# The prompt's output projection of a hybrid decoder step, cut by half the columns and a quarter of the rows instead of a quarter and a half, inside the page steps

## The chip, the cores and the metric

One Trainium2 chip, one of its cores. The metric is the device time of one launch in microseconds; the median of 3 runs of the kernel before is 806.1 us (802.2 to 810.11). The engines are called TensorE (PE, and PEld for its weight loads), VectorE (DVE), ScalarE (ACT), GpSimd (POOL) and SyncE (SP).

## What is computed

One step of a decoder layer for a prompt of 512 tokens and for 8 sample sequences of 4 tokens each, which look back on 4096 cached tokens. Each layer projects the input, runs a recurrent group and an attention group with three branches (compressed, selected, sliding window), gates both, concatenates them and projects the result back. What the change touches is this:

```
s = jnp.einsum('bkgtd,bjkd->bkgtj', q, kc[:, :, 0]) * ATTN_SCALE        # compressed_attn, sample: keys from the cache pages
...
o = g[0] * o_c + g[1] * o_s + g[2] * o_w
o = o.transpose(0, 3, 1, 2, 4).reshape(B, T, N_WIDTH).astype(y_r.dtype) * jax.nn.silu(gate_n)
return jnp.concatenate([y_r, o], axis=-1) @ w_out                       # mixer_out
...
y = x + mixer_out(y_r, o_c, o_s, o_w, gl, gate_n, w_out)                # prompt_layer: 512 x 1024 times 1024 x 1024
...
y_prompt = rms_norm(y_p, final_g)
```

## The kernel before

The launch has three stages: the input projection and the recurrent group (to about 330 us), the prompt's attention with the rest of the recurrent group (to about 536 us), and then the stage that the change touches.

**Page steps.** The samples' cache is read page by page by an indirect DMA that GpSimd issues (`load_page`, L1328 to L1332). A step s = 8b + i takes page i of sequence b, 64 steps in all; I call the eight steps of a sequence a batch. Four page buffers hold the pages (NPAGE), and step s issues the load of page s + 4 when its own page is no longer read. The order of the work on TensorE, VectorE, ScalarE and GpSimd is written out by hand (`manual_schedule`, L1714), and each engine runs its instructions in that order. SyncE's queue, which carries the plain loads and stores, is ordered by a scheduler.

In each step `keys` (L1690) turns the page's selected keys (`ks_set`, L1394) and compressed keys (`kc_set`, L1373): four TensorE transposes of 128 x 128 each into one of three PSUM banks, from which ScalarE copies the former (`kts`) and VectorE the latter (`ktc`; in step 3 ScalarE). `keep_values` copies the page's values away (`vt`, on ScalarE in even steps, on VectorE in odd ones). `scores` multiplies the compressed keys of two pages in every odd step (`kc_mm`, L1384 to L1391), the selected keys of four pages in steps 3 and 7 (`ks_mm`, L1407), and at the end of a batch copies the compressed scores out of PSUM (`top1`, `sc`, L1414).

`chain` and `chain_early` then do for sequence b - 1, spread over the steps of batch b, what follows from its scores: the selection (`top2`, `top2b`, `top3`: L1420 to L1448, with the block scores `bs` on VectorE), the penalty (`top4`, L1455 to L1467, whose matmuls at L1457 need `bs`, and VectorE's copies `pe` at L1460), the softmax (L1476 to L1486), the transposes of the weights (`weights`, L1492, copied as `p` by ScalarE and VectorE), the products with the values (L1504, L1519, L1530) and their reduction (`values_r`, `Rc`, L1512).

**The prompt's output projection** runs in the same steps. The product is made in split precision: a weight piece is copied to a high part by ScalarE and its remainder made by GpSimd (`o_split`, L1551, tile WHL), a piece of the gated input G is split the same way by ScalarE and VectorE (`o_prep`, L1561, tile CHL), and TensorE adds high x high, low x high and high x low in PSUM (`o_mm`, L1567). There are 8 units u of 256 columns (u // 2) and half of the rows (u % 2), each with 8 calls of `o_mm`: four blocks i of 128 tokens, each in two parts c of two row tiles, six matmuls of 256 columns a call. After the second part VectorE adds the bank to Y (L1575), and after the second half of the rows ScalarE sums the squares (L1577). `output_step` (L1581) gives a unit nine steps: its split in the first, a call in each of the other eight, and the piece for a call is made one step before it:

```
        u, r = divmod(s, 9)
        if r == 0: o_split(u)
        if r < 8:  o_prep(u, r)
        if r:      o_mm(u, r - 1)
```

So 72 steps are needed: 64 page steps hold units 0 to 6 and the split of unit 7, and the eight calls of unit 7 lie in the eight steps after the last page. With each second call of unit 7 `final(i)` (L1595 to L1602) normalises a token block: two small VectorE steps, a power on GpSimd, one VectorE product with the gain vector `fgt`, and the store. The gain vector is loaded by unit 7's split over the weight buffer WS.

**The tail.** After the last page step the chain of the last sequence runs in eight steps without pages, each followed by `output_step`; then `join` combines the branches of all sequences (L1610 to L1658) and the samples' projection and normalisation end the launch (L1758 to L1769). The weights for it (WO) are loaded into the page buffers.

The functions that the diff touches, with the lines of the profile:

## Time and profile before

| | |
|---|---|
| median of 3 runs | 806.1 us (802.2 to 810.11) |
| profiled execution | 805.09 us |
| its span, first to last instruction | 803.3 us |
| mean granted TensorE clock | 0.948 of 2.4 GHz |
| busy: TensorE, VectorE, ScalarE, GpSimd | 719.6, 515.4, 341.8, 293.5 us |

Times are microseconds from the span's start unless marked ns. A row of a timeline gives the start, the busy time, the engine, the line, the operation, the tile written and the tiles read, the shapes and the number of instructions merged; in brackets stands how long the engine had been idle and what ended that. Matmuls are pipelined and their ends modelled, so that the distance of two starts says more than one duration.

### The profile page before, as it was taken

The numbers are of one execution on the slowest core, as the hardware profiler recorded it, in microseconds if no ns is written. First come the engines' busy times: TensorE is split into PE (matmuls) and PEld (weight loads), VectorE is DVE, ScalarE is ACT, GpSimd is POOL, SyncE is SP. The second block draws the span as 40 slices with busy tenths as digits, with TensorE's granted clock in tenths as the row PEclk, the third lists the DMA queues.
The fourth block names the chain that finished last, engine by engine and source line by source line (L and its number), as shares of the span: only waits on it lengthen the run. The fifth ranks groups of instructions, "written<-read, shape, count | busy, mean of one in ns | idle before, by whom it ended". The sixth has DMA issues, their size and how long they took to land.

```text
span 803.3 us, 17119 instructions
## 1 busy us (share of the span) xinstructions
PE 719.6 (90%) x6922; PEld 602.2 (75%) x6922; DVE 515.4 (64%) x1236; ACT 341.8 (43%) x731; POOL 293.5 (37%) x323
## 2 busy tenths in 40 slices
PE   3997988998899999699999999988989999998775
PEld 2896977888787999598888787665757766676553
DVE  7687587779921520867766665855776666667653
ACT  5335635542021223234544343455554664656420
POOL 5276566554231164500011023224443554434100
PEclk9998998999799899769999999999999999999977
DMA  7733233265373133311115100389888889898841
GB/s 212 264 90 99 63 95 95 53 169 111 81 157 88 29 105 79 119 21 27 28 27 133 27 8 1 127 294 369 301 326 286 304 321 312 299 344 321 253 126 60
DMA packets 103912, 125.01 MB, mean 156 GB/s; under 512 B 59085, under 2 KB 90551, under 8 KB 95386
## 3 DMA queue, kind: packets, MB, share of 16 engines
q1 hardware_dynamic: 94074, 56.48, 26.4%
q0 software_dynamic: 9216, 67.11, 23.0%
q8 instruction: 54, 0.88, 0.4%
q10 hardware_dynamic: 544, 0.33, 0.2%
q14 instruction: 24, 0.20, 0.1%
HBM read 112.81 MB, written 15.26 MB: 159 GB/s over the span
## 4 chain that ended last, share of the span: by engine, by line
PE 61%; DVE 18%; DMA 10%; issue 5%; ACT 4%; POOL 2%; SPq 1%; POOLq 0%; DVEq 0%; ACTq 0%
PE bx L366 16%; DMA pg<-in_cache_kv_dram,idx 5%; PE bn L1256 2%; PE bn L1571 2%; PE ba L1391 2%; PE bt L1001 2%; PE bn L1250 2%; PE bt L1398 2%; PE bn L1519 2%; PE bn L1504 2%; PE bt L1009 1%; DVE LT L566 1%; PE bn L1231 1%; DVE CHL L1565 1%; PE bt L1381 1%
## 5 line engine op out<-in xcount | busy, mean ns | idle before, releaser
L366 PE MATMUL bx<-xh,WR 128*128 128x272 f32 x992 | 182.9, 300 | 2.6 <-POOL WR L360 2.3
L366 PEld LDWEIGHTS bx<-xh,WR 128*128 128x128 f32 x992 | 149.7, 197 | 6.2 <-POOL WR L360 2.7
L366 PE MATMUL bx<-xl,WR 128*128 128x272 f32 x496 | 110.5, 299 | 0.0
L1332 POOL DMA_INDIRECT pg<-in_cache_kv_dram,idx x64 | 62.6, 978 | 119.1 <-PE bn L1530 18.3
L360 POOL TENSOR_TENSOR WR<-WA,WR 128x1024 fp32r<-128x1024 f32 x31 | 76.1, 2454 | 70.5 <-ACT WR L114 70.3
L366 PEld LDWEIGHTS bx<-xl,WR 128*128 128x128 f32 x496 | 83.3, 198 | 0.9
L1571 PE MATMUL bn<-WHL,CHL 128*128 128x256 f32 x384 | 64.8, 304 | 3.9 <-DVE CHL L1565 2.6
L1571 PEld LDWEIGHTS bn<-WHL,CHL 128*128 128x128 f32 x384 | 51.7, 195 | 8.6 <-DVE CHL L1565 4.3
L114 ACT ACTIVATE WR<-WA 128x1024 fp32r<-128x1024 f32 x31 | 32.7, 1056 | 57.6 <-PE bx L366 26.7
L1382 DVE COPY ktc<-bt 128x512 f32<-128x512 f32 x38 | 26.1, 687 | 32.4 <-PE bt L1381 32.4
L1025 POOL TENSOR_TENSOR std<-st,DC 128x512 f32<-128x512 f32 x7 | 7.3, 1049 | 99.5 <-DVE st L1051 37.6
L1565 DVE TENSOR_TENSOR CHL<-G,CHL 128x256 fp32r<-128x256 f32 x64 | 32.2, 503 | 17.1 <-ACT CHL L114 17.1
L1235 ACT ACTIVATE pr<-bn,nm 128x128 f32<-128x128 f32 (+3 forms) x57 | 28.8, 507 | 26.1 <-PE bn L1250 12.1
L1391 PE MATMUL ba<-ktc,WA 128*32 128x255 f32 x512 | 34.0, 383 | 6.3 <-DVE ktc L1382 4.7
L114 ACT ACTIVATE kts<-bt 128x512 f32<-128x512 f32 x43 | 25.5, 593 | 31.1 <-PE bt L1398 31.1
L1234 DVE TENSOR_REDUCE nm<-bn 128x1 f32<-128x128 f32 (+3 forms) x57 | 26.0, 461 | 7.1 <-PE bn L1233 6.7
L1555 POOL TENSOR_TENSOR WHL<-WA,WHL 128x512 fp32r<-128x512 f32 x16 | 21.1, 1338 | 25.7 <-ACT WHL L114 25.7
L1398 PEld LDWEIGHTS bt<-ident,pg 128*128 128x128 f32 x172 | 18.6, 140 | 15.0 <-issue 10.0
L114 ACT ACTIVATE vt<-pg 128x1024 f32<-128x1024 f32 x28 | 29.4, 1048 | 0.0
L1398 PE MATMUL bt<-ident,pg 128*128 128x128 f32 x172 | 27.4, 282 | 2.1 <-DMA pg<-in_cache_kv_dram,idx 2.0
L1256 PE MATMUL bn<-ps,VP 128*64 128x128 f32 x320 | 27.4, 287 | 1.2 <-ACT ps L114 1.0
L1391 PEld LDWEIGHTS ba<-ktc,WA 128*32 128x32 f32 x512 | 14.3, 109 | 18.0 <-DVE ktc L1382 5.2
(544 smaller groups left out, 1774.7 us busy)
## 6 DMA issues: line engine op xcount, KB each, us to landing
WA<-in_w_in_dram SPq DMA_DIRECT2D x23, 512.0 KB
WA<-in_w_in_dram SPq DMA_DIRECT2D x16, 256.0 KB
vt<-in_cache_kv_win_dram SPq DMA_DIRECT2D x8, 512.0 KB
out_dram<-in_cache_kv_win_dram SPq DMA_DIRECT2D x8, 508.0 KB
...
```

The costliest lines, as they stand in the source:

```text
L114: return act(o, i, AF.Copy, scale=scale)
L360: ptt(lo[:, :, :n], src[:, :, :n], h[:, :, :n], op=OP.subtract)
L366: mm(z[:, u, 0:HT], w[:, t, :], x[u][:, t, :], start=first, stop=last)
L1234: red(nm[:, k:k + 1], S[:, 0:n], axis=AX.X, op=OP.max, negate=True)
L1235: act(pr[:, k, 0:n], S[:, 0:n], AF.Exp, bias=nm[:, k:k + 1], accum_out=l2[:, k:k + 1])
L1256: mm(OT[64 * k:64 * k + 64, g, :], VP[:, br, t0 + t, 64 * k:64 * k + 64], ps[:, (2 * t + k) * P:(2 * t + k + 1) * P], start=False, stop=(b ...
L1332: nc.gpsimd.indirect_dma_start(out=t, out_offset=None, in_=cache_rows, in_offset=bass.IndirectOffsetOnAxis(ap=idx[:, 2 * b + c_t:2 * b + c ...
L1382: (acopy if i == 3 and b else cp)(KCT[b, q][:, :, c_t, :], pt.rearrange("p (t c) -> p t c", t=4))
L1391: mm(SCB[r, 0:255], QW[:, 4 * q + t, m, :], kt[:, t].rearrange("p a c -> p (a c)")[:, m:m + 255], start=(q == 0 and t < 2), stop=(q == 3 a ...
L1398: tp(pt[:, t * P:(t + 1) * P], PG[b, i][:, t, 2, :], ident)
L1565: tt(CHL[c][:, 1], cat, CHL[c][:, 0], op=OP.subtract)
L1571: mm(YB[:, 0:256], CHL[c][:, x, t], WHL[:, w, 2 * c + t], start=(c + t + x + w == 0), stop=(c + t == 2 and w == 1))
```

## The change

The projection goes by half the columns (512, h = u // 4) and a quarter of the rows (two row tiles, r = u % 4). A unit has four calls, one for each token block, of six matmuls of 512 columns; the bank is added to Y after each. `OSTEP` names the steps of the calls: the odd steps for units 0 to 5, and steps 49 to 52 and 54 to 57 for units 6 and 7. The splits come at steps 0, 8, 16, 24, 32, 40, 48 and 53, and the four `final(i)` at steps 59 to 62, so that nothing of it is left after the last page. In `keys` the compressed keys are transposed before the selected ones.

```diff
-    WHL = w2.tile([P, 2, 4, 256], F32R, name="WHL")
+    WHL = w2.tile([P, 2, 2, 512], F32R, name="WHL")
...
-    WS = WA[:, 1024:2048].rearrange("p (t c) -> p t c", t=4)
-    def load_wo(w, n, cols, c0):
-        if n < 4:
-            nc.sync.dma_start(w, dram(w_out, n * P * D + c0, [[D, P], [P * D, 4], [1, cols]]))
+    WS = WA[:, 1024:2048].rearrange("p (t c) -> p t c", t=2)
+    def load_wo(w, r, cols, c0):
+        if r < 2:
+            nc.sync.dma_start(w, dram(w_out, 2 * r * P * D + c0, [[D, P], [P * D, 2], [1, cols]]))
...
     def o_load(u):
-        load_wo(WS, 4 * (u % 2), 256, 256 * (u // 2))
+        load_wo(WS, u % 4, 512, 512 * (u // 4))
     def o_split(u):
-        for c in range(2):
-            t = slice(2 * c, 2 * c + 2)
+        for t in range(2):
             acopy(WHL[:, 0, t], WS[:, t])
             ptt(WHL[:, 1, t], WS[:, t], WHL[:, 0, t], op=OP.subtract)
...
-    def o_prep(u, n):
-        i, c = n // 2, n % 2
-        cat = G[:, 4 * (u % 2) + 2 * c:4 * (u % 2) + 2 * c + 2, i * P:(i + 1) * P]
-        acopy(CHL[c][:, 0], cat)
-        tt(CHL[c][:, 1], cat, CHL[c][:, 0], op=OP.subtract)
-    def o_mm(u, n):
-        (q, h), (i, c) = divmod(u, 2), divmod(n, 2)
+    def o_prep(u, i):
+        cat, hl = G[:, 2 * (u % 4):2 * (u % 4) + 2, i * P:(i + 1) * P], CHL[i % 2]
+        acopy(hl[:, 0], cat)
+        tt(hl[:, 1], cat, hl[:, 0], op=OP.subtract)
+    def o_mm(u, i):
+        h, r = divmod(u, 4)
         for t in range(2):
             for x, w in ((0, 0), (1, 0), (0, 1)):
-                mm(YB[:, 0:256], CHL[c][:, x, t], WHL[:, w, 2 * c + t], start=(c + t + x + w == 0),
-                   stop=(c + t == 2 and w == 1))
-        if c:
-            y = Y[i][:, 256 * q:256 * q + 256]
-            tt(y, YB[:, 0:256], y, op=OP.add)
-            if h:
-                act(YB[:, 256:512], y, AF.Square, accum_out=ssq[:, i, q:q + 1])
-            if u == 7:
-                final(i)
+                mm(YB, CHL[i % 2][:, x, t], WHL[:, w, t], start=(t + x + w == 0), stop=(t == 1 and w == 1))
+        y = Y[i][:, 512 * h:512 * h + 512]
+        tt(y, YB, y, op=OP.add)
+        if r == 3:
+            act(YB, y, AF.Square, accum_out=ssq[:, i, h:h + 1])
+    OSTEP = {}
+    for u in range(8):
+        for i in range(4):
+            OSTEP[8 * u + 2 * i + 1 if u < 6 else 48 + 5 * (u - 6) + i + 1] = (u, i)
     def output_step(s):
-        u, r = divmod(s, 9)
...
+        if s in (0, 8, 16, 24, 32, 40, 48, 53):
+            o_split(len([x for x in (8, 16, 24, 32, 40, 48, 53) if x <= s]))
+        if s + 1 in OSTEP:
+            o_prep(*OSTEP[s + 1])
+        if s in OSTEP:
+            o_mm(*OSTEP[s])
+        if 59 <= s < 63:
+            final(s - 59)
...
     def keys(b, i):
+        kc_set(b, i)
         ks_set(b, i)
-        kc_set(b, i)
...
         for i in range(8):
             chain_early(B - 1, i)
             chain(B - 1, i)
-            output_step(8 * B + i)
```

The loads of WO for the samples' projection use the new `load_wo` and move the same bytes.

On TensorE, the first three steps of a batch in the middle of the page steps, before (L1398 are the selected keys' transposes, L1381 the compressed keys', L1571 a call of the projection, L1420 and L1442 matmuls of the selection, L1391 the compressed scores, L1455 and L1457 the penalty):

```order
L1398 MATMUL bt_68<-ident,pg 128x128 x4
L1381 MATMUL bn_3255<-ident,pg 128x128 x4
L1571 MATMUL bn_3252<-WHL,CHL_5415 128x256 x6
L1420 MATMUL bn_3253<-sc,selR 32x255
L1398 MATMUL bt_67<-ident,pg 128x128 x4
L1381 MATMUL bt_68<-ident,pg 128x128 x4
L1571 MATMUL bn_3252<-WHL,CHL_5414 128x256 x6
L1391 MATMUL ba_69<-ktc,WA 32x255 x8
L1442 MATMUL bn_3253<-bw,s_6423 8x65
L1398 MATMUL bn_3255<-ident,pg 128x128 x4
L1381 MATMUL bt_67<-ident,pg 128x128 x4
L1571 MATMUL bn_3252<-WHL,CHL_5415 128x256 x6
```

and now, where the projection's call has L1570:

```order
L1381 MATMUL bt_68<-ident,pg 128x128 x4
L1398 MATMUL bn_3255<-ident,pg 128x128 x4
L1420 MATMUL bn_3253<-sc,selR 32x255
L1381 MATMUL bt_67<-ident,pg 128x128 x4
L1398 MATMUL bt_68<-ident,pg 128x128 x4
L1570 MATMUL bn_3252<-WHL,CHL_5414 128x512 x6
L1391 MATMUL ba_69<-ktc,WA 32x255 x8
L1442 MATMUL bn_3253<-bw,s_6345 8x65
L1381 MATMUL bn_3255<-ident,pg 128x128 x4
L1398 MATMUL bt_67<-ident,pg 128x128 x4
L1455 MATMUL bn_3253<-kvsm,qbd 32x32 x4
L1457 MATMUL bn_3253<-bs,rep_3541 128x32 x2
```

The compressed keys' transposes stand first, the calls of steps 0 and 2 are gone, and the call of step 1 has 512 columns.

On VectorE, in the tail, from the block scores of the last sequence to its softmax (L1448 removes the found maxima from `bs`, L1565 is the piece of G for a call, L1575 the update of Y, L1597 to L1601 the normalisation, L1460 and L1461 the copies of the penalty, L1476 the softmax), before:

```order
L1448 MATCH_REPLACE bs<-v_8138,bs 8x65
L1565 TENSOR_TENSOR CHL_5414<-G,CHL_5414 128x256
L1575 TENSOR_TENSOR Y_5409<-bn_3252,Y_5409 128x256
L1597 TENSOR_REDUCE ss<-ssq 128x1
L1598 TENSOR_SCALAR ss<-ss 128x1
L1601 SCALAR_TENSOR_TENSOR Y_5409<-Y_5409,rs,WA 128x1024
L1460 TENSOR_SCALAR pe<-bn_3253 128x32
L1461 COPY pe<-bn_3253 128x32
L1476 ISA sp,m_8175<-pe,tailm 128x32
```

and now:

```order
L1447 MAX v_7964<-bs 8x8
L1448 MATCH_REPLACE bs<-v_7964,bs 8x65
L1460 TENSOR_SCALAR pe<-bn_3253 128x32
L1461 COPY pe<-bn_3253 128x32
L1476 ISA sp,m_7984<-pe,tailm 128x32
L1476 ISA m_7984 128x1
```

All of the projection and the normalisation between the block scores and the copies of the penalty is gone from there. On ScalarE and GpSimd each split's two high copies and two subtractions keep their order within a step; the splits of units 1 to 6 now stand in step 0 of a batch, that of unit 7 in step 5.

## Rows read from the trace of the kernel before

**Rows 1.** The page's first part: busy time, share of the span and number of instructions of each engine, over the whole span.

```profile
PE 719.6 (90%) x6922; PEld 602.2 (75%) x6922; DVE 515.4 (64%) x1236; ACT 341.8 (43%) x731; POOL 293.5 (37%) x323
```

**Rows 2.** The windows view: two stretches, one of page steps and the tail. Columns: stretch, its length, busy time and number of instructions of PE, PEld, DVE, ACT and POOL, PE's granted clock as a share of full speed, mean busy share of the DMA engines, GB/s.

```profile
673.00:701.00 28.00, 26.14 (x315) 19.36 (x314) 19.80 (x49) 16.62 (x34) 13.29 (x15) 1.00 0.85 309
...
759.00:804.00 45.00, 27.36 (x320) 18.93 (x318) 21.40 (x68) 7.74 (x25) 2.78 (x5) 0.78 0.36 102
```

**Rows 3.** The view of one source line: VectorE's copy of the compressed scores at the end of each batch, with min/median/max duration in ns and the first and last start.

```profile
L1414 DVE COPY sc<-ba x8: 409/423/425, 555.5 to 758.2; 128x255 f32<-128x255 f32 x8
```

**Rows 4.** TensorE's timeline of one batch (b = 5): the first transposes of its eight steps and of the next batch's first (L1398), and the matmuls of steps 0, 2 and 7 that the text speaks of.

```profile
672.79 0.66 PE L1398 MATMUL bt<-ident,pg 128*128 128x128 f32 x4
...
673.64 0.96 PE L1571 MATMUL bn<-WHL,CHL 128*128 128x256 f32 x6
674.53 0.62 PE L1420 MATMUL bn<-sc,selR 128*32 128x255 f32 x2
675.53 0.66 PE L1398 MATMUL bn<-ident,pg 128*128 128x128 f32 x4 [0.38 <-DMA pg<-in_cache_kv_dram,idx]
...
678.64 0.66 PE L1398 MATMUL bt<-ident,pg 128*128 128x128 f32 x4
...
680.57 0.63 PE L1457 MATMUL bn<-bs,rep 8*128 8x32 f32 x4
...
682.12 0.63 PE L1398 MATMUL bt<-ident,pg 128*128 128x128 f32 x4 [0.68 <-DMA pg<-in_cache_kv_dram,idx]
...
686.55 0.66 PE L1398 MATMUL bt<-ident,pg 128*128 128x128 f32 x4
...
691.26 0.60 PE L1398 MATMUL bt<-ident,pg 128*128 128x128 f32 x4
...
694.57 0.65 PE L1398 MATMUL bt<-ident,pg 128*128 128x128 f32 x4
...
696.21 0.60 PE L1398 MATMUL bn<-ident,pg 128*128 128x128 f32 x4
...
698.90 1.07 PE L1391 MATMUL ba<-ktc,WA 128*32 128x255 f32 x16 [0.72 <-DVE ktc L1382]
...
700.76 0.66 PE L1398 MATMUL bt<-ident,pg 128*128 128x128 f32 x4
```

**Rows 5.** The timeline: a call of the projection and what follows it on TensorE; and, earlier, two 512-column matmuls with weights of the same type (L1231, L1232) and what follows them.

```profile
540.54 0.96 PE L1571 MATMUL bn<-WHL,CHL 128*128 128x256 f32 x6
...
541.34 0.60 PE L1398 MATMUL bt<-ident,pg 128*128 128x128 f32 x4
...
505.62 0.48 PE L1231 MATMUL ba<-WR,QR 128*128 128x512 f32 x1
505.94 0.40 PE L1232 MATMUL ba<-WR,QR 128*128 128x512 f32 x1
506.17 0.23 PE L1233 MATMUL ba<-causb,identb 128*128 128x128 bf16 x1
```

**Rows 6.** The timeline at a split of the projection's weights: ScalarE's two high copies, GpSimd's two subtractions, VectorE's subtraction of G's piece beside them; and that subtraction at another split.

```profile
692.39 1.14 ACT L114 ACTIVATE WHL<-WA 128x512 fp32r<-128x512 f32 x2
...
693.09 2.70 POOL L1555 TENSOR_TENSOR WHL<-WA,WHL 128x512 fp32r<-128x512 f32 x2 [2.97 <-ACT WHL L114]
...
693.87 0.78 DVE L1565 TENSOR_TENSOR CHL<-G,CHL 128x256 fp32r<-128x256 f32 x1 [0.77 <-ACT CHL L114]
...
593.95 2.95 DVE L1565 TENSOR_TENSOR CHL<-G,CHL 128x256 fp32r<-128x256 f32 x1 [0.28 <-ACT CHL L114]
```

**Rows 7.** ScalarE's timeline in step 4 of the same batch: the copy of the transposed weights.

```profile
688.88 0.60 ACT L114 ACTIVATE p<-bn 128x512 f32<-128x512 f32 x1
```

**Rows 8.** The waits view for TensorE, from 536 to 759: waiting line, what it waited for, us in total, times, the longest.

```profile
PE ba L1391 <- DVE ktc L1382: 4.7, 7, 1.3
PE bn L1571 <- DVE CHL L1565: 2.6, 3, 1.8
```

**Rows 9.** The view of the page loads' line: issue to landing.

```profile
DMA to landing us min/median/max: 5.4/7.6/10.5
```

**Rows 10.** VectorE's timeline in the tail.

```profile
758.24 0.41 DVE L1414 COPY sc<-ba 128x255 f32<-128x255 f32 x1
...
760.70 0.43 DVE L1565 TENSOR_TENSOR CHL<-G,CHL 128x256 fp32r<-128x256 f32 x1 [0.93 <-ACT CHL L114]
...
768.79 1.28 DVE L1601 SCALAR_TENSOR_TENSOR Y<-Y,rs,WA 128x1024 f32<-128x1024 f32 x1 [3.34 <-DMA WA<-in_final_g_dram]
769.99 0.18 DVE L1460 TENSOR_SCALAR pe<-bn 128x32 f32<-128x32 f32 x1
...
776.34 1.28 DVE L1601 SCALAR_TENSOR_TENSOR Y<-Y,rs,WA 128x1024 f32<-128x1024 f32 x1 [0.67 <-POOL rs L1600]
777.54 0.68 DVE L1494 COPY p<-bn 128x512 f32<-128x512 f32 x1
...
780.99 0.27 DVE L1615 TENSOR_TENSOR p2t<-mn,bt 8x128 f32<-8x128 f32 x1 [1.44 <-PE bn L1530]
```

**Rows 11.** TensorE's timeline in the tail (the penalty's matmuls) and the windows view of two stretches of it, columns as in rows 2.

```profile
763.91 1.06 PE L1457 MATMUL bn<-bs,rep 8*128 8x32 f32 x4 [0.33 <-DVE bs L1448]
...
764.00:774.00 10.00, 6.56 (x37) 4.93 (x38) 4.93 (x17) 2.67 (x7) 0.57 (x1) 0.50 0.66 176
774.00:791.00 17.00, 14.15 (x227) 10.42 (x225) 11.81 (x31) 3.40 (x12) 1.67 (x3) 1.00 0.16 64
```

More of the change, by code (lines that the diff above doesn't have):

```diff
@@ L1533, in tile_hymba_step @@
     TOP, P2, VT, PM = {}, {}, {}, {}
[L1536 to L1541 removed]
+    WS = WA[:, 1024:2048].rearrange("p (t c) -> p t c", t=2)
+    def load_wo(w, r, cols, c0):
+        if r < 2:
+            nc.sync.dma_start(w, dram(w_out, 2 * r * P * D + c0, [[D, P], [P * D, 2], [1, cols]]))
         else:
             for k in range(2):
[L1544 removed]
+                nc.sync.dma_start(w[64 * k:64 * k + 64],
+                                  dram(w_out, (256 + 256 * k + 128 * r) * D + c0, [[D, 64], [64 * D, 2], [1, cols]]))
     def o_load(u):
[L1549 removed]
+        load_wo(WS, u % 4, 512, 512 * (u // 4))
     def o_split(u):
[L1552 to L1553 removed]
+        for t in range(2):
             acopy(WHL[:, 0, t], WS[:, t])
@@ L1559, in o_split @@
             nc.sync.dma_start(fgt, dram(final_g, 0, [[0, P], [1, D]]))
[L1561 to L1568 removed]
+    def o_prep(u, i):
[4 more added lines that the diff above has]
+        h, r = divmod(u, 4)
         for t in range(2):
             for x, w in ((0, 0), (1, 0), (0, 1)):
[L1571 to L1592 removed]
+                mm(YB, CHL[i % 2][:, x, t], WHL[:, w, t], start=(t + x + w == 0), stop=(t == 1 and w == 1))
[7 more added lines that the diff above has]
+            OSTEP[8 * u + 2 * i + 1 if u < 6 else 48 + 5 * (u - 6) + i + 1] = (u, i)
+    def output_step(s):
+        if s in (0, 8, 16, 24, 32, 40, 48, 53):
[6 more added lines that the diff above has]
+            final(s - 59)
+    ssq = small.tile([P, 4, 2], F32, name="ssq", bufs=1)
     fgt = WA[:, 1024:2048]
@@ L1730, in tile_hymba_step @@
         for i in range(4):
-            if i < 2:
-                nc.sync.dma_start(WO[i], dram(w_out, 2 * i * P * D, [[D, P], [P * D, 2], [1, D]]))
-            else:
-                for k in range(2):
-                    nc.sync.dma_start(WO[i][64 * k:64 * k + 64],
-                                      dram(w_out, (512 + 256 * k + 128 * (i - 2)) * D, [[D, 64], [64 * D, 2], [1, D]]))
+            load_wo(WO[i], i, D, 0)
         for i in range(8):
```

10 lines of the change are left out of this document (removed).

## The prediction

> **What bounds the kernel now.** I read the page's busy shares first [rows 1]: TensorE 90%, far above VectorE's 64%, so TensorE comes first; but a share over the whole span mixes stages, so I looked at the two stages that the change touches, through the windows [rows 2]. In the page steps TensorE is busy 26.14 of 28 us at the full clock; in the tail, after the last page step, 27.36 of 45, at 0.78. So the page steps are mostly TensorE work, and the tail is a chain of waits. The copy of the compressed scores that closes each batch of eight steps starts at 555.5 for the first batch and at 758.2 for the last [rows 3], so a batch takes 202.7 / 7 = 28.96 us. The starts of TensorE's first transposes give the steps of one batch [rows 4]: 2.74, 3.11, 3.48, 4.43, 4.71, 3.31, 1.64 and 4.55, sum 27.97. The tail is read further down, from VectorE's timeline.
>
> **The change, part by part.**
>
> *The projection's matmuls.* Six 256-column matmuls start at 540.54 and what follows them at 541.34 [rows 5]: 0.80 us a call, 64 calls. A 512-column matmul with the same kind of weights is followed after 0.32 by a second, and that after 0.23 by the next instruction [rows 5]: the first of a group pays some 0.08 more. Six are 0.32 + 5 x 0.24 = 1.5 us, for 32 calls. In all 64 x 0.80 = 51.2 becomes 48.0. Had the width brought nothing it would be 51.2; were every one of the six 0.23, it would be 44.2. But now all 32 lie in page steps, where 56 of the 64 lay before: 44.8 becomes 48.0 there.
>
> *The batches 1 to 5 of page steps.* In the batch of [rows 4] I take out seven calls (5.6), and the three waits that it shows, 0.38, 0.68 and 0.72, each with about 0.25 that the mark leaves out because it counts from the modelled end of the matmul before: 2.5. What remains is 27.97 - 5.6 - 2.5 = 19.9 us. Four calls of 1.5 make it 25.9. To that come gaps. The odd steps now hold projection and compressed scores; the even ones hold no projection, and VectorE's and ScalarE's short chains, which a call covered in each step, lie open there. I laid the new order beside the durations, by hand:
> - Steps 0 to 1. Each split now falls on step 0. ScalarE has a score copy and a key copy before it (as long as the copy of [rows 7]; I estimate it free 1.6 us after the step's first transposes), then the two high copies, 1.14 [rows 6], and the copy of G's piece, some 0.35: 3.1. VectorE's subtraction beside GpSimd's takes 0.78 [rows 6]: 3.9. TensorE has two steps' transposes (0.85 each) and the 0.62 of the selection's first matmul [rows 4]: 2.3. Gap 1.6.
> - Step 2. The penalty matmul starts 1.93 after its step [rows 4] and waits for nothing long, since transposes and a call lie ahead of it. Without the call TensorE comes at 1.05, and the block scores are ready no sooner than about 1.8 (my estimate), as the wider Y update stands before them on VectorE. Gap 0.75.
> - Step 4. ScalarE's copy of the weights starts 2.33 after the step and takes 0.60 [rows 7, 4]; with a CHL copy now always ahead of it, it is done at 3.4 to 3.5. TensorE comes to it at 2.8 instead of 3.6. Gap 0.7.
> - Steps 6 to 7. The subtraction made in step 6 is ready at about 2.4; TensorE, with 1.7 of transposes, waits 0.7.
> The sum is 25.9 + 3.75 = 29.65, against 28.96: +0.69 for each of five batches, +3.4. The swapped keys are in it: the copy of the compressed keys now ends before the projection does, so its waits, 4.7 us in all [rows 8], can at most become nothing; but in step 7, where [rows 4] has one, the late CHL piece takes the place. I give the swap nothing beyond that. Pages are no new limit here: one lands 7.6 us after its issue, 10.5 at most [rows 9], and each is asked for four steps ahead.
>
> *First batch and last two.* The first has no chain and pays the step 6 gap at light steps: +0.7. Batch 6 takes seven calls instead of four, 4.5 us more, of which the gaps of steps 2 and 4 hide part and a split in step 5 costs little: +1.5 against 28.96. Batch 7 loses all calls after step 1, but its steps 3 to 6 take the four final normalisations on VectorE, each 1.28 for the product and about 0.9 for its small steps, 0.67 of it the wait for GpSimd's power [rows 10], 8.8 us in order with the key copies: -0.5 against 29.2. Page steps in all: 3.4 + 0.7 + 1.5 - 0.5 = +5.1. From below: all the gaps covered is 25.9 a batch, -3.1 x 5, and then -13.8 for the page steps; from above: a subtraction of 2.95 [rows 6] in place of 0.78 at each of six splits, +13.0 more.
>
> *The tail.* It runs from the score copy at 758.24 to the end. Unit 7 and the normalisations leave it. Four stalls on VectorE go [rows 10]:
> - the CHL subtraction at 760.70, with its wait for ScalarE's copy, ahead of the next step of the selection: 0.6;
> - the penalty copy at 769.99. Its matmuls start at 763.91 and take 1.06 [rows 11], so it could run at 765.1; it stood behind a product that waited 3.34 for the gain vector's load, issued only in unit 7's split: 4.9;
> - the copy of the last weights at 777.54, behind a Y update, two small steps, a wait of 0.67 and a product of 1.28: 2.4;
> - in the join, from 780.99 on, two Y updates, a CHL subtraction (0.4 each) and a third product of 1.28: 2.5.
> Sum 10.4. What is late next is TensorE itself. The granted clock is 0.50 from 764 to 774 and 1.00 until 791 [rows 11]; in the half-rate stretch the penalty matmuls take 1.06, at the full clock 0.63 [rows 11, 4]. The work that moves ahead of 774 when the stalls go (transposes of the weights, half the compressed and half the selected values) is what step 4 holds beside its transposes and its call, 4.71 - 0.85 - 0.80 = 3.06 [rows 4]; at half rate it costs as much again: +3.0. So the tail gains 7.4. Bounds: 10.4 if the clock is full all along, 3.4 if all of some 7 us of its matmuls ran at half.
>
> *Sum.* The profiled execution took 805.09 us (span 803.3 and 1.8 around it): 805.09 + 5.1 - 7.4 = 802.8. It stands 1.0 below the median 806.1, so I say 803.8, rounded 804.
>
> **A rule against the change.** VectorE's subtraction took 0.78 beside GpSimd's pair of 2.70, and once 2.95 [rows 6]. The Trainium skill, page "SBUF — State Buffer", section "Who interferes with whom", says that a VectorE instruction with two SBUF inputs and a GpSimd instruction that reads SBUF lock each other out for a whole instruction. The trace agrees: 0.78 is the rest of one half, 2.95 a wait for both. By the rule the price depends on which arrives first, so the new place of the split may pay 2.95 each time.
>
> **The rivals.**
> - *The gaps are covered.* If the chains come early enough that half of each gap closes (for it: the key copies are freed sooner, ScalarE has half as many CHL copies; against it: the order on ScalarE in step 0 is fixed), a batch takes 27.8, 1.9 less than above, over six batches 11.4: 804 - 11.4 = 792.6.
> - *The split stalls at every batch: slower.* One mechanism: the subtraction of step 0 waits for both of GpSimd's halves, 2.95 instead of 0.78, 2.17 more at each of six splits, 13.0 us: 804 + 13.0 = 817. It decides (over 1%) from five of the six splits on. For it: it happened at 593.95, and now step 0 has the least other work on TensorE. Against: TensorE's waits for CHL are 2.6 us in all before [rows 8].
> - *The tail keeps its length.* If the clock stays at half, the tail gains 3.4 and the page steps give it back: 808.
>
> **How the numbers follow.** A measurement of this kernel tells about 1%, 8 us, from no change: faster means below 798, slower above 814.2. The forecast (798 to 812 as its own range) 0.45, the kept tail 0.08, covered gaps 0.28, the stalled split 0.19. So within 1%: 0.53; faster 0.28; slower 0.19. The range reaches to the covered gaps and to the stalled split: 792 to 817; outside it I leave what lies beyond either, under 2 in 10.
>
> **What would show it.** Right: batches of 29 to 30 us between score copies; no wait of the compressed scores for their key copy in steps 1, 3 and 5; TensorE idle before the first call of steps 1 and 7, and before the penalty matmul of step 2; no wait for the gain vector; a tail of 37 to 39 us. Wrong: batches under 28 (the gaps were covered), subtractions of some 3 us at the splits, or a clock of 0.50 within the page steps, and a tail over 42.

## The result: 0.7% slower

The changed kernel took 810.0 us (median of 20 executions, 806.1 to 815.0), the kernel before 804.4 (20 executions, 799.2 to 810.1): ratio 1.0069, 95% interval 1.0049 to 1.0089. The forecast was 804. The profiled execution took 813.16 (span 811.4); before it was 805.09. The profiled execution of the changed kernel is the fourth slowest of its 20, so its rows show a loss of 8.1 us where the medians show 5.7.

The page's busy shares (as in [rows 1]) tell next to nothing of it: TensorE is at 90% as before.

```profile
PE 728.0 (90%) x6730; PEld 588.6 (73%) x6730; DVE 509.9 (63%) x1204; ACT 330.4 (41%) x683; POOL 290.4 (36%) x323
```

The copies of the compressed scores ("score copies" from here), which close the batches (as in [rows 3]):

```profile
L1414 DVE COPY sc<-ba x8: 416/423/424, 557.9 to 771.1; 128x255 f32<-128x255 f32 x8
```

The first comes 2.4 us later than before, the last 12.8 later. One by one, the seven batches take 31.58, 29.81, 29.83, 29.84, 29.82, 32.52 and 29.75, where they took 28.96 in the mean (27.67 to 30.72 one by one). The tail, from the last score copy to the end, takes 40.3 instead of 45.0, so 12.8 - 4.7 = 8.1 are lost. The windows of a steady batch, of batches 6 and 7 and of the tail (columns as in [rows 2]):

```profile
679.00:708.80 29.80, 28.03 (x299) 18.16 (x295) 19.37 (x48) 15.02 (x28) 12.87 (x14) 1.00 0.84 301
708.80:741.30 32.50, 30.66 (x315) 20.42 (x307) 22.49 (x52) 18.29 (x36) 15.96 (x16) 1.00 0.80 286
741.30:771.10 29.80, 23.88 (x283) 16.45 (x283) 22.27 (x56) 14.91 (x29) 7.66 (x10) 0.99 0.92 321
771.10:811.40 40.30, 25.10 (x280) 13.96 (x272) 12.40 (x46) 4.39 (x11) 0.54 (x1) 0.63 0.33 88
```

The steady batch (b = 5) on TensorE: the first transposes of its eight steps and of the next batch's first (L1381, two rows in step 6 to 7), and the matmuls that wait. This answers to [rows 4].

```profile
679.70 0.66 PE L1381 MATMUL bt<-ident,pg 128*128 128x128 f32 x4
...
681.27 0.66 PE L1381 MATMUL bn<-ident,pg 128*128 128x128 f32 x4
...
682.87 0.50 PE L1570 MATMUL bn<-WHL,CHL 128*128 128x512 f32 x1 [0.51 <-ACT CHL L114]
683.67 1.66 PE L1570 MATMUL bn<-WHL,CHL 128*128 128x512 f32 x5 [0.30 <-DVE CHL L1564]
...
686.46 0.66 PE L1381 MATMUL bt<-ident,pg 128*128 128x128 f32 x4
...
694.07 0.66 PE L1381 MATMUL bt<-ident,pg 128*128 128x128 f32 x4
...
697.65 1.08 PE L1519 MATMUL bn<-vt,p 128*32 128x128 f32 x32 [0.39 <-issue]
...
698.78 0.60 PE L1381 MATMUL bt<-ident,pg 128*128 128x128 f32 x4
...
704.40 0.60 PE L1381 MATMUL bn<-ident,pg 128*128 128x128 f32 x4
...
707.65 1.07 PE L1391 MATMUL ba<-ktc,WA 128*32 128x255 f32 x16 [0.15 <-DVE ktc L1382]
...
709.51 0.66 PE L1381 MATMUL bt<-ident,pg 128*128 128x128 f32 x4
```

Step 1 takes 5.19, step 4 4.71, step 7 5.11. In each, a matmul waits for something that comes, directly or through VectorE, from ScalarE: step 1 for the attention piece, step 4 for ScalarE's copy of the weights (the row here names no releaser), step 7 for a key copy that stands behind the next piece on VectorE. The waits view of TensorE over the page steps (536 to 771, columns as in [rows 8]) has all three, beside the pages:

```profile
PE bn L1570 <- ACT CHL L114: 3.7, 6, 1.2
PE bt L1381 <- DMA pg<-in_cache_kv_dram,idx: 3.7, 3, 2.0
PE ba L1391 <- DVE ktc L1382: 3.0, 6, 2.2
PE bn L1570 <- DVE CHL L1564: 1.8, 6, 0.3
...
PE bn L1519 <- ACT p L114: 1.2, 3, 0.4
```

### The profile page after: what moved, and what is told of

Same layout as the page of the kernel before. It is cut to its first block, busy times and chain, and to the rows that moved or that the text cites. A ratio compares the mean times of both kernels' runs of the same rounds, so it can differ in the third digit from the quotient of the medians.

```text
span 811.4 us, 16645 instructions
## 1 busy us (share of the span) xinstructions
PE 728.0 (90%) x6730; PEld 588.6 (73%) x6730; DVE 509.9 (63%) x1204; ACT 330.4 (41%) x683; POOL 290.4 (36%) x323
## 4 chain that ended last, share of the span: by engine, by line
PE 59%; DVE 16%; issue 9%; DMA 6%; ACT 5%; POOL 2%; SPq 1%; POOLq 0%; ACTq 0%; DVEq 0%
PE bx L366 14%; PE bn L1570 3%; PE bn L1256 3%; PE bt L1001 2%; PE bn L1250 2%; DMA pg<-in_cache_kv_dram,idx 2%; PE ba L1391 2%; PE bt L1009 1%; PE bt L1381 1%; PE bt L1398 1%; PE bn L1519 1%; DVE LT L566 1%; DMA out_dram<-in_cache_kv_win_dram 1%; PE bn L1231 1%; PE bn L1504 1%
## 5 line engine op out<-in xcount | busy, mean ns | idle before, releaser
L1570 PE MATMUL bn<-WHL,CHL 128*128 128x512 f32 x192 | 58.2, 427 | 6.8 <-ACT CHL L114 3.7
L1570 PEld LDWEIGHTS bn<-WHL,CHL 128*128 128x128 f32 x192 | 34.4, 193 | 21.1 <-ACT CHL L114 6.8
L1025 POOL TENSOR_TENSOR std<-st,DC 128x512 f32<-128x512 f32 x7 | 7.3, 1048 | 99.4 <-DVE st L1051 37.6
L1235 ACT ACTIVATE pr<-bn,nm 128x128 f32<-128x128 f32 (+3 forms) x57 | 28.8, 507 | 27.0 <-PE bn L1250 12.9
L1391 PE MATMUL ba<-ktc,WA 128*32 128x255 f32 x512 | 34.1, 383 | 3.0 <-DVE ktc L1382 3.0
L1564 DVE TENSOR_TENSOR CHL<-G,CHL 128x256 fp32r<-128x256 f32 x32 | 18.6, 580 | 27.9 <-ACT CHL L114 27.8
L1381 PE MATMUL bt<-ident,pg 128*128 128x128 f32 x172 | 27.6, 283 | 3.7 <-DMA pg<-in_cache_kv_dram,idx 3.7
L1381 PEld LDWEIGHTS bt<-ident,pg 128*128 128x128 f32 x172 | 18.6, 141 | 16.7 <-issue 12.0
L1572 DVE TENSOR_TENSOR Y<-bn,Y 128x512 f32<-128x512 f32 x32 | 21.9, 685 | 12.6 <-PE bn L1570 12.6
L1256 PE MATMUL bn<-ps,VP 128*64 128x128 f32 x320 | 27.9, 288 | 1.0 <-ACT ps L114 0.9
```

What stands on the lines that cost most here:

```text
L1235: act(pr[:, k, 0:n], S[:, 0:n], AF.Exp, bias=nm[:, k:k + 1], accum_out=l2[:, k:k + 1])
L1256: mm(OT[64 * k:64 * k + 64, g, :], VP[:, br, t0 + t, 64 * k:64 * k + 64], ps[:, (2 * t + k) * P:(2 * t + k + 1) * P], start=False, stop=(b ...
L1381: tp(pt[:, t * P:(t + 1) * P], PG[b, i][:, t, 0, :], ident)
L1391: mm(SCB[r, 0:255], QW[:, 4 * q + t, m, :], kt[:, t].rearrange("p a c -> p (a c)")[:, m:m + 255], start=(q == 0 and t < 2), stop=(q == 3 a ...
L1570: mm(YB, CHL[i % 2][:, x, t], WHL[:, w, t], start=(t + x + w == 0), stop=(t == 1 and w == 1))
L1572: tt(y, YB, y, op=OP.add)
```

## The experiments

Fifteen runs, of 4 to 10 executions each; each ratio is to the kernel before on the same chip, with its 95% interval, and is the safer figure where two runs are compared, since they come from several chips. "Batch" is the mean of batches 2 to 5 between score copies in the profiled execution, "last score copy" and "tail" are from that execution too.

| run | median us | ratio | batch | last score copy | tail |
|---|---|---|---|---|---|
| before | 804.4 | 1 | 28.7 | 758.2 | 45.0 |
| after | 810.0 | 1.0069 (1.0049 to 1.0089) | 29.8 | 771.1 | 40.3 |
| swap_back | 804.4 | 1.0017 (0.9997 to 1.0037) | 28.6 | 760.5 | 37.0 |
| swap_only | 810.9 | 1.0109 (1.0034 to 1.0185) | 29.2 | 763.1 | 41.8 |
| scalar_pad | 809.1 | 1.0054 (1.0016 to 1.0091) | 29.7 | 772.0 | 36.8 |
| engines_exchanged | 798.1 | 0.9920 (0.9888 to 0.9952) | 28.4 | 761.7 | 35.5 |
| ex_before | 803.3 | 0.9985 (0.9962 to 1.0007) | 28.6 | 756.0 | 43.8 |
| split_early | 819.4 | 1.0206 (1.0172 to 1.0239) | 32.3 | 782.6 | 34.3 |
| halves | 809.9 | 1.0108 (1.0051 to 1.0165) | 30.1 | 769.4 | 40.1 |
| back_halves | 806.2 | 1.0030 (0.9994 to 1.0065) | 30.1 | 763.6 | 37.3 |
| ex_halves | 802.1 | 0.9967 (0.9934 to 1.0001) | 29.2 | 759.1 | 35.4 |
| finals_tail | 812.1 | 1.0098 (1.0062 to 1.0134) | 29.9 | 768.4 | 43.0 |
| back_two | 801.7 | 0.9974 (0.9930 to 1.0018) | 28.6 | 762.3 | 37.3 |
| ex_two | 796.4 | 0.9916 (0.9885 to 0.9946) | 28.4 | 758.8 | 35.0 |
| ex_spread | 800.2 | 0.9956 (0.9926 to 0.9986) | 28.4 | 756.2 | 42.0 |
| ex_two_prep | 799.2 | 0.9950 (0.9916 to 0.9983) | 28.3 | 755.8 | 35.4 |
| narrow_8 | 811.4 | 1.0090 (1.0055 to 1.0125) | 29.4 | 766.2 | 40.8 |

### Is it the swap of the two transposes?

**swap_back**, the changed kernel with the swap undone:

```diff
     def keys(b, i):
-        kc_set(b, i)
         ks_set(b, i)
+        kc_set(b, i)
```

> The changed kernel with the selected keys transposed first again, as before the change. Theory (the swap is worth next to nothing; the loss is in where the projection's calls lie): the compressed scores wait longer for their key copy (3.0 us in all in the changed kernel, 4.7 before), batches 2 to 5 stay at 29.8 to 30.2, 811 to 815 against the changed kernel's 810 to 813. Rival (the swap is what slows the page steps, since the copy of the selected keys on ScalarE now starts half a us later and everything on ScalarE behind it): batches near 29.0, 804 to 807.

The rival was right. The steady batch fell from 29.83 to 28.6, the median by 5.6 us, and the ratio to the kernel before from 1.0069 to 1.0017, which is not clear of no change. TensorE's first transposes of steps 1, 2, 4, 5 and 7 of batch 5, and of the next batch, in that kernel:

```profile
671.80 0.66 PE L1398 MATMUL bn<-ident,pg 128*128 128x128 f32 x4
...
676.51 0.66 PE L1398 MATMUL bt<-ident,pg 128*128 128x128 f32 x4
...
684.11 0.66 PE L1398 MATMUL bt<-ident,pg 128*128 128x128 f32 x4
...
688.39 0.60 PE L1398 MATMUL bt<-ident,pg 128*128 128x128 f32 x4
...
694.00 0.60 PE L1398 MATMUL bn<-ident,pg 128*128 128x128 f32 x4
...
698.82 0.66 PE L1398 MATMUL bt<-ident,pg 128*128 128x128 f32 x4
```

Step 1 takes 4.71 instead of 5.19, step 4 4.28 instead of 4.71, step 7 4.82 instead of 5.11: together 1.20 of the 1.22 by which batch 5 differs. The other five steps are as long as in the changed kernel to within 0.02.

**swap_only**, the kernel before with the two calls swapped, the same edit the other way round.

> The kernel before with one thing changed: compressed keys transposed first. Theory (a later ScalarE costs only where a step has no projection to cover it, and the narrow scheme has a call in nearly every step): batches within 0.3 of the 28.96 of before, total within 2 us of before, 802 to 806. Rival (the swap costs 1.2 a batch whatever the scheme): batches 29.8 to 30.4, 809 to 813. A gain is possible too: the compressed scores wait 4.7 us for their key copy in all, which would give 799 to 801.

The theory that the narrow scheme's calls cover it fell by the time: 810.9, as the rival had it. The rival's 1.2 a batch is not what the rows show, though: batches 2 to 5 take 29.16 instead of 28.73 in the mean (27.05 to 32.07 one by one). Most of what is lost there lies in the first batch: from the first transposes of the page steps (519.31, before 521.52) to the first score copy it takes 38.6 instead of 34.0. Its profiled execution was its fastest of four (806.74), so how the narrow scheme pays the rest is not shown.

### By which engine?

The swap puts the transposes that ScalarE copies second, about half a us later in a step. ScalarE's timeline in step 0 of batch 5 of the changed kernel (step begins at 679.70):

```profile
679.86 0.60 ACT L114 ACTIVATE sp<-ba 128x512 f32<-128x512 f32 x1 [2.68 <-PE ba L1407]
680.87 0.60 ACT L114 ACTIVATE kts<-bt 128x512 f32<-128x512 f32 x1 [0.42 <-PE bt L1398]
681.37 1.14 ACT L114 ACTIVATE WHL<-WA 128x512 fp32r<-128x512 f32 x2
682.41 0.41 ACT L114 ACTIVATE CHL<-G 128x256 fp32r<-128x256 f32 x1
```

and in swap_back (step begins at 670.22):

```profile
670.39 0.60 ACT L114 ACTIVATE sp<-ba 128x512 f32<-128x512 f32 x1 [2.84 <-PE ba L1407]
670.92 0.60 ACT L114 ACTIVATE kts<-bt 128x512 f32<-128x512 f32 x1
671.41 1.14 ACT L114 ACTIVATE WHL<-WA 128x512 fp32r<-128x512 f32 x2
672.45 0.41 ACT L114 ACTIVATE CHL<-G 128x256 fp32r<-128x256 f32 x1
```

The key copy starts 1.17 after the step's start in the one, with ScalarE idle for 0.42 ahead of it until TensorE has the transposes done, and 0.70 in the other; the copy of the projection's piece (CHL, "attention piece" in these texts) starts at 2.71 and 2.23. The 0.48 go straight into step 1's wait.

**engines_exchanged** leaves the compressed keys first and gives their copy to ScalarE:

```diff
-        (acopy if i == 3 and b else cp)(KCT[b, q][:, :, c_t, :], pt.rearrange("p (t c) -> p t c", t=4))
+        (cp if i == 3 and b else acopy)(KCT[b, q][:, :, c_t, :], pt.rearrange("p (t c) -> p t c", t=4))
...
-        acopy(kt, pt.rearrange("p (t c) -> p c t", t=4))
+        (acopy if i == 3 and b else cp)(kt, pt.rearrange("p (t c) -> p c t", t=4))
```

> The changed kernel, compressed keys still first, but with the engines of the two key copies exchanged: ScalarE copies the compressed keys and VectorE the selected ones. Theory (the swap costs because ScalarE's queue opens with the copy of the selected keys, and starts 0.45 us later in each step, with all its other copies behind it): ScalarE is as early as with the selected keys first, batches 2 to 5 fall from 29.83 to 28.5 to 28.8, 803 to 806. Rival (it is the order on TensorE itself, or the later selected keys): batches stay at 29.6 to 30, 809 to 813.

Batches 28.4, just under the theory's range, and the time was well below it: 798.1, 0.8% under the kernel before. Steps 1, 4 and 7 take 4.71, 4.27 and 4.58.

**ex_before**, swap_only with the same exchange of engines:

> The kernel before with compressed keys transposed first and with the engines of the two key copies exchanged (ScalarE copies the compressed keys, VectorE the selected ones). Theory (the swap costs by ScalarE's later start, in the narrow scheme as in the wide one): the 8 us by which the swap alone slowed the kernel before go away: 799 to 804. Rival (in the narrow scheme the swap costs in another way): 807 to 812.

803.3: the loss of swap_only is gone.

**scalar_pad**, swap_back with ScalarE alone made later:

```diff
         kt = KS[b, i] = sa.tile([P, P, 4], F32, name="kts", bufs=NKS)
+        acopy(small.tile([P, 400], F32, name="pad", bufs=1), pt[:, 0:400])
         acopy(kt, pt.rearrange("p (t c) -> p c t", t=4))
```

> The changed kernel with the selected keys first again, and with a copy of 400 columns on ScalarE ahead of each copy of the selected keys, whose result nothing uses: some 0.4 us by which that copy and all behind it on ScalarE come later in each step, while the order on TensorE and VectorE stays. Theory (the swap costs by ScalarE's later start alone): batches 2 to 5 rise from 28.62 to 29.4 to 30.2, 809 to 814. Rival (the swap costs by the order on TensorE or VectorE, and ScalarE, busy half of the time, has room): 28.6 to 28.9, 803 to 806.

Its ScalarE in step 0 of batch 5 (step begins at 679.35), and its TensorE in step 1 (L1571 is the projection there):

```profile
679.51 0.60 ACT L114 ACTIVATE sp<-ba 128x512 f32<-128x512 f32 x1 [2.29 <-PE ba L1408]
680.09 0.50 ACT L114 ACTIVATE pad<-bt 128x400 f32<-128x400 f32 x1
680.49 0.59 ACT L114 ACTIVATE kts<-bt 128x512 f32<-128x512 f32 x1
...
682.01 0.41 ACT L114 ACTIVATE CHL<-G 128x256 fp32r<-128x256 f32 x1
...
682.48 0.50 PE L1571 MATMUL bn<-WHL,CHL 128*128 128x512 f32 x1 [0.46 <-ACT CHL L114]
```

The pad moves the key copy to 1.14 after the step's start and the piece's copy to 2.66. Steps 1, 4 and 7 take 5.15, 4.67 and 5.06, the batch 29.70, the whole 809.1 (its interval overlaps swap_back's, the batches do not). With the order on TensorE and VectorE as in swap_back, ScalarE's delay alone gives the changed kernel's batch back. That settles the cause of the longer steady batches.

### Are the gaps of steps without a call to be covered?

**halves** cuts each call of units 0 to 5 in two, three matmuls in the odd step and three in the next:

```diff
-    def o_mm(u, i):
+    def o_mm(u, i, ts_=(0, 1)):
         h, r = divmod(u, 4)
-        for t in range(2):
+        for t in ts_:
...
     def output_step(s):
+        if s - 1 in OSTEP and OSTEP[s - 1][0] < 6:
+            o_mm(*OSTEP[s - 1], (1,))
...
-            o_mm(*OSTEP[s])
+            o_mm(*OSTEP[s], (0,) if OSTEP[s][0] < 6 else (0, 1))
```

> The changed kernel with each call of units 0 to 5 cut in two: three 512-column matmuls in the odd step, three in the even step behind it, so that every step has some. Theory (steps without a call leave the chains of VectorE and ScalarE open: in a steady batch the penalty's, the compressed values' and step 6's transposes own about 0.4, 0.6 and 0.9 us more than their least): half to all of that is covered, less 24 more group starts of about 0.08: batches 28.5 to 29.0, first batch to batch 5 give 5 to 7 us: 804 to 808. Rival (the time lost in a batch hangs on the split's place and on the regular length of odd steps, not on cover): batches 29.5 to 29.9, 809 to 812.

**back_halves** is halves on top of swap_back.

> The changed kernel with the selected keys first again and each call of units 0 to 5 cut into three matmuls in the odd step and three in the even step behind it. Theory (with ScalarE early, what is left of the gaps is the penalty's 0.4 and the compressed values' 0.2 a batch, and three more for the first call): batches 2 to 5 28.0 to 28.4, 801 to 803.5. Rival (the extra group starts eat it): 28.6 to 29.0, 804 to 807.

Both missed in the total. Batches 1, 2 and 5 are as the theory had them (28.5 to 28.8; 27.9 to 28.2), but batches 3 and 4 took 31.4 to 32.2. ScalarE and TensorE of back_halves in step 7 of batch 3 show one reason:

```profile
635.70 0.60 ACT L1576 ACTIVATE bn<-Y 128x512 f32<-128x512 f32 x1 [1.21 <-DVE Y L1574]
...
636.33 0.40 ACT L114 ACTIVATE CHL<-G 128x256 fp32r<-128x256 f32 x1
...
636.78 1.19 PE L1570 MATMUL bn<-WHL,CHL 128*128 128x512 f32 x3 [0.97 <-ACT CHL L114]
```

The square of unit 3 now stood ahead of the next piece's copy on ScalarE and waited for VectorE's update. **ex_halves** (on top of engines_exchanged) prepares the piece first:

> The changed kernel with exchanged copies, calls of units 0 to 5 cut into three matmuls in the odd step and three in the even step, and in each step the next attention piece prepared ahead of the second three and of the split (so that no square stands ahead of it on ScalarE). Theory (cover in even steps is worth the 0.5 a batch that it showed in the undisturbed batches, and the two batches of 32 were made by the squares): batches 1 to 5 27.6 to 28.1, 794 to 797. Rival (batches 3 and 4 stay at 31 to 32 for another reason): 798 to 803.

Batches 1, 2 and 5 are 27.9 to 28.3, batches 3 and 4 shorter but still 30.5 and 29.8, so the total is the rival's and the squares were only part of the reason; the rest was not followed. In the undisturbed batches cover is worth 1.2 where ScalarE is late (28.5 to 28.8 against 29.83) and 0.5 where it is early (27.9 to 28.2 against 28.6): so about half of it was cover for the swap.

**split_early** puts each split one step earlier, behind the last call of the unit before:

```diff
-        if s in (0, 8, 16, 24, 32, 40, 48, 53):
-            o_split(len([x for x in (8, 16, 24, 32, 40, 48, 53) if x <= s]))
...
+        if s in (0, 7, 15, 23, 31, 39, 47, 52):
+            o_split(len([x for x in (7, 15, 23, 31, 39, 47, 52) if x <= s]))
```

> The changed kernel with each split of the weights one step earlier, behind the last call of the unit before (steps 7, 15, 23, 31, 39, 47, 52 in place of 8, 16, 24, 32, 40, 48, 53), and behind its step's own attention piece. Theory (the split's copies on ScalarE and its subtractions on GpSimd stand ahead of the first call's attention piece; 0.81 us of marked wait a batch, about 1.1 by the starts): the wait before the first call of step 1 goes, batches 2 to 5 fall from 29.83 to 28.7 to 29.0, 7 splits give 5 to 7 us: 803 to 807. Rival (ScalarE and GpSimd are as late in step 7, where two score and key copies and the next queries wait for them): batches stay at 29.6 to 30, 809 to 813.

It was the slowest of all, 819.4, and neither theory named the reason. GpSimd and TensorE about its steps 31 to 35:

```profile
653.67 2.51 POOL L1555 TENSOR_TENSOR WHL<-WA,WHL 128x512 fp32r<-128x512 f32 x2 [1.84 <-ACT WHL L114]
656.32 0.97 POOL L1332 DMA_INDIRECT pg<-in_cache_kv_dram,idx  x1
...
664.94 1.08 PE L1381 MATMUL bt<-ident,pg 128*128 128x128 f32 x4 [2.95 <-DMA pg<-in_cache_kv_dram,idx]
```

The page requests are on GpSimd's queue. In step 31, which TensorE began at 648.45, the request stood behind a split that waited for ScalarE's copies; these overwrite the old weights, and so come only after the unit's last call; it left at 656.32, and step 35 waited 2.95 for that page, 8.6 later. From 536 to 771 TensorE waits 13.8 us for pages, against 5.4 in the changed kernel.

### The packed end

**finals_tail** takes the normalisations out of steps 59 to 62 and puts them in the tail's steps 3 to 6.

> The changed kernel with its four final normalisations moved out of page steps 59 to 62 into steps 3 to 6 of the tail. Theory (they block VectorE in batch 7: 8 us of them in order with the key copies): batch 7 falls from 29.75 to 26 to 27.5, and the tail, 40.3, gets 2 to 4 longer since VectorE idles there most of the time: 808 to 811. Rival (batch 7 is set by the pages' arrival, and the normalisations lay in waiting time): batch 7 stays over 29, the tail grows by 3 to 6: 813 to 818.

Windows of batch 7 and the tail (columns as in [rows 2]):

```profile
741.20:768.40 27.20, 25.34 (x283) 16.96 (x283) 16.79 (x43) 14.74 (x29) 5.36 (x6) 0.94 0.90 309
768.40:811.40 43.00, 24.76 (x280) 14.86 (x272) 17.91 (x58) 4.39 (x11) 3.07 (x5) 0.66 0.40 110
```

Batch 7 fell by 2.5 as the theory had it, and the tail grew by 2.7: the normalisations cost about the same on either side. The time, 812.1, lies between the theory's range and the rival's.

**back_two** (on swap_back) and **ex_two** (on engines_exchanged) cut the normalisation in two, the power a step ahead of the product:

```diff
-    def final(i):
+    def final_a(i):
...
         ptt(rs, ss, mhalf[:, 0:1], op=OP.pow)
+        RS[i] = rs
+
+    def final(i):
+        rs = RS.pop(i)
         stt(Y[i], Y[i], rs, fgt, op0=OP.mult, op1=OP.mult)
...
+        if 58 <= s < 62:
+            final_a(s - 58)
```

> The changed kernel with the selected keys first again, and the four final normalisations cut in two: sums and GpSimd's power in steps 58 to 61, the wide product a step later, so that VectorE no longer waits for GpSimd between them (0.69, 1.24, 0.44 and 0.66 us). Theory (batch 7 is set by VectorE with the normalisations in order): batch 7 falls from 31.2 to 28.5 to 29.7, 801 to 803.5. Rival (the pages' arrival sets it, or the power stands behind a page request on GpSimd wherever it is put): batch 7 over 30.3, 803.5 to 805.

> The changed kernel with exchanged copies and with the final normalisations cut in two, power a step ahead of the wide product. Theory (VectorE's waits for GpSimd's power, 3.0 us, lie half on the path of batch 7): batch 7 falls from 29.85 to 28.3 to 29.3, 796 to 797.5. Rival (batch 7 is held by page arrival or by the order of the products with the key copies): no change, 797.5 to 799.

VectorE in the changed kernel's batch 7, the four products:

```profile
754.37 1.28 DVE L1601 SCALAR_TENSOR_TENSOR Y<-Y,rs,WA 128x1024 f32<-128x1024 f32 x1 [0.69 <-POOL rs L1600]
...
758.68 1.28 DVE L1601 SCALAR_TENSOR_TENSOR Y<-Y,rs,WA 128x1024 f32<-128x1024 f32 x1 [1.24 <-POOL rs L1600]
759.88 0.68 DVE L1494 COPY p<-bn 128x512 f32<-128x512 f32 x1
...
763.37 1.29 DVE L1601 SCALAR_TENSOR_TENSOR Y<-Y,rs,WA 128x1024 f32<-128x1024 f32 x1 [0.65 <-POOL rs L1600]
...
766.90 1.28 DVE L1601 SCALAR_TENSOR_TENSOR Y<-Y,rs,WA 128x1024 f32<-128x1024 f32 x1 [0.66 <-POOL rs L1600]
```

The second power stands behind a page request on GpSimd (the request from 757.03, the power from 758.05), so VectorE waits 1.24, and the copy of the weights with it. With the power a step ahead, batch 7 fell from 29.85 to 27.53 in ex_two, more than expected, and from 30.83 to 29.93 in back_two, between the theory's range and the rival's. ex_two is the fastest here, 0.84% under the kernel before, though its interval overlaps that of engines_exchanged.

**ex_spread** (on engines_exchanged) gives units 6 and 7 a call in every second step as the others, `OSTEP[8 * u + 2 * i + 1]` throughout, and the normalisations to the tail:

> The changed kernel with exchanged copies and without the packing at the end: units 6 and 7 have a call in every second step as the others, up to step 63, and the four final normalisations stand in steps 3 to 6 of the tail. Theory (packing moves work between batches 6 and 7 and the tail, and wins only the tail's waits for the normalisations): batch 6 28.4, batch 7 29.5 to 31, tail 2 to 3 longer: 798 to 801. Rival (packed calls and normalisations in the page steps cost more than they save): 794 to 797.

800.2, in the theory's range. Batches 2 to 7 took 28.3 to 28.4, the seventh less than expected, and the tail 42.0. So, against engines_exchanged, packing costs 31.43 - 28.34 = 3.1 in batch 6 and 29.85 - 28.34 = 1.5 in batch 7, and gives 42.0 - 35.5 = 6.5 in the tail.

### Width and the split's order

**narrow_8**, the kernel before with `divmod(s, 8)` for 9 in `output_step`, so that its narrow calls end at the tail's first step:

> The kernel before, 256-column calls and selected keys first, but with eight steps to a unit instead of nine: the calls run through without a break, the last one and its last normalisation come in the tail's first step, the other three normalisations in steps 58, 60 and 62. It has the change's shorter tail without its wider calls. Theory (what the change gives, apart from the swap, is the tail; the wider calls give 0.1 us a call pair and lose it again in the steps without a call): 7 more calls of 0.80 in page steps, tail 6 to 8 shorter: 800 to 804. Rival (a call in every step covers so much that it beats the wide calls outright): 795 to 799. If the width is what counts: 804 to 808.

811.4, slower than each case expected. Up to the fifth, batches of 30.1 and 28.7 alternate, and batch 7, with its eight calls and three normalisations, took 35.7. The narrow calls pay more in the page steps than the shorter tail (40.8) gives.

**ex_two_prep**, ex_two with the attention piece prepared ahead of the split:

> The changed kernel with exchanged copies, the final normalisations cut in two, and in the steps with a split the attention piece prepared ahead of the split, on ScalarE and VectorE. Theory (the piece's subtraction then runs beside ScalarE's weight copies and before GpSimd's subtractions; the wait of 0.3 before the second matmul of step 1 goes, and some of that before the first): 0.3 to 0.8 a split, seven splits: 791 to 795. Rival (the first matmul waits for the weights' high copies anyway, which come later by the piece's copy): no change, 796 to 798.

799.2, above both ranges. The theory's 0.3 to 0.8 a split isn't there: the steady batch is 28.33 against 28.37. Its executions spread from 792.9 to 805.2, so the time itself decides nothing.

## Why the prediction was wrong, step by step

*The swap: the step that failed.* The text said that the swap is in the gaps, that it can only remove the 4.7 us of waits for the key copy, and "I give the swap nothing beyond that". That counted only the copy which gets earlier. The one that gets later heads ScalarE's queue. The hand-laid gaps had ScalarE late already (free 1.6 after the step's start; it was 1.67, and 1.19 in swap_back), so the steady batch came out nearly right, 29.65 against 29.83, and hid whose cost it was: 1.2 a batch is the swap's, and without it the wide scheme's batch (28.6) is as short as before. Two runs bound the mechanism from both sides: ScalarE early with the swap in place (engines_exchanged), and late without it (scalar_pad).

Undoing the swap took 5.6 us out of the medians. The profiles show more, but part of it is no effect of the swap: swap_back's execution came to the page steps 2.2 us earlier, over stages that are the same in both kernels. These are the first transposes of the page steps, in the changed kernel and then in swap_back:

```profile
521.47 0.60 PE L1381 MATMUL bt<-ident,pg 128*128 128x128 f32 x4
```

```profile
519.24 0.60 PE L1398 MATMUL bt<-ident,pg 128*128 128x128 f32 x4
```

From there to the last score copy it is 249.6 and 241.3, so the page steps got 8.3 shorter; in the kernel before (from 521.52) they take 236.7. Swapped back, the page steps are thus 4.6 longer than before and the tail 8.0 shorter, where the forecast had 5.1 and 7.4. That agreement is luck, and errors cancel in it: the forecast has +0.7 for a steady batch where swap_back has -0.3, and +1.5 and -0.5 for batches 6 and 7 where it has +2.6 and +1.9.

*The sum.* Forecast for the profiled execution 802.8, measured 813.16. Of the 10.4 us between them, the tail has 2.7 and the page steps 7.7: the first batch 1.7, batch 1 1.9, batches 2 to 5 0.7, batch 6 2.1, batch 7 1.3.

*The gaps.* Steps 0 to 1, 2, 4 and 6 to 7 were named, and in the changed kernel these have the waits. But the penalty's and the weights' gaps (0.75 and 0.7) showed marked waits of 0.37 and 0.39, and the compressed scores in step 7 wait not for "the late CHL piece" itself but for a key copy that stands behind it on VectorE.

*The calls.* Six 512-column matmuls take 1.57 (689.78 to what follows at 691.35) against 1.5. If all 32 are as this one, they take 50.2 and not 48.0, and the width saved 1 us of 51.2 and not 3.2.

*First batch and batch 1.* Forecast +0.7 and +0.7, measured +2.4 and +2.6. Little of the first is the swap's: from the first transposes to the first score copy it is 34.0 before, 36.4 in the changed kernel and still 35.9 in swap_back. In the changed kernel TensorE waits for pages, 4.3 us in steps 5, 7 and 9, and behind the longest of these waits, 2.0 in step 9, the granted clock was 0.50 (1.2 GHz) from 562.5 to 565.5. That is not the same in every execution: finals_tail, which is the same kernel up to step 58, waits 2.7 us for pages there, and its batch 1 takes 29.68 and not 31.58. Why the pages came late was not followed.

*Batch 6.* Forecast 30.5, measured 32.5. Three more calls took 2.7 on top of the steady batch; the forecast's 30.5 leaves them 0.8 over its own steady batch of 29.65. Its 1.5 was added to the old batch, 28.96, and the gaps hid less of the calls than it assumed.

*Batch 7.* Forecast 28.7, measured 29.75. The normalisations were priced at 0.67 of waiting each; one waited 1.24 behind a page request, and where the waits are taken out (ex_two) batch 7 takes 27.53 instead of 29.85. The 29.2 from which the forecast took off 0.5 stands in no row shown, and its sum counts from 28.96.

*The tail.* Forecast -7.4, measured -4.7 in this execution. The stalls went: VectorE's copy of the penalty's values comes 7.4 after the score copy instead of 11.75 [rows 10], that of the last weights 13.1 instead of 19.3, and the gain vector is waited for no more. What was lost is the clock: 1.00 of it is 2.4 GHz, 0.50 is 1.2 GHz, and what lies between is a mean of stretches at either. From the join's first VectorE instruction (as in [rows 10]) to the end, in the changed kernel and then in swap_back, whose tail has the same instructions:

```profile
789.60:811.40 21.80, 11.48 (x143) 6.57 (x143) 4.29 (x18) 1.06 (x4) 0.54 (x1) 0.61 0.03 7
```

```profile
777.90:797.50 19.60, 9.31 (x143) 5.60 (x143) 4.29 (x18) 1.06 (x4) 0.54 (x1) 0.78 0.03 8
```

The same 32 matmuls of the join, at 1.2 GHz in the changed kernel and at 2.4 in swap_back:

```profile
791.34 3.51 PE L1752 MATMUL bt<-pg,G 128*32 128x256 f32 x32 [0.41 <-DVE gw L1632]
```

```profile
779.64 1.93 PE L1752 MATMUL bt<-pg,G 128*32 128x256 f32 x32 [0.41 <-DVE gw L1632]
```

At a mean granted clock of 0.78 the stretch is the 22.3 - 2.5 = 19.8 of the forecast; at 0.61 it is 2.2 longer. swap_back's and scalar_pad's whole tails are 37.0 and 36.8, against 37.6 forecast. So the tail was sized well for that clock. Whether the changed kernel's other executions have fewer half-rate stretches there isn't shown: its mean clock over the whole launch goes from 0.938 to 0.952 in the 20, and is 0.941 in the profiled one; but halves, with the same order of the keys, also has a tail of 40.1.

*The rivals.* No subtraction of a piece took 2.95: the longest of 32 was 0.86, so the stalled split didn't happen. The kept tail came half: 4.7 gained in the profiled execution, between its 3.4 and the forecast's 7.4, but 8.0 and 8.2 in swap_back and scalar_pad. The rule of the Trainium skill (page "SBUF — State Buffer", section "Who interferes with whom") shows as 0.77 beside GpSimd's halves, as before, and as 0.72 to 0.86 in step 2 of batches 1 to 5, beside GpSimd's multiplication for the queries (L1368), where a subtraction with neither beside it takes 0.42. The 2.95 of before began while such a multiplication ran (593.53 to 594.15), with both halves right behind it; in the changed kernel GpSimd waits 0.72 for ScalarE between the two (to 682.07 in batch 5). The gaps were not covered, by what the text had against it, ScalarE's order in step 0: a batch takes 28.4 in engines_exchanged, where ScalarE is early, against that rival's 27.8. The result lies within the 1% that was held likeliest, but on the other side.

*What stays open.* swap_back and engines_exchanged have the same span in the profile (797.5 and 797.2), but medians of 804.4 and 798.1 (ratios 1.0017 and 0.9920). swap_back's profiled execution was its fastest, and had the early start above: from the first transposes to the end it takes 278.3 against 275.4. That is 2.9 of the difference; what swap_back's other executions spend more was not seen.
